# Token gathers of a mixture of experts take the list with out-of-range empty slots and skip them

## The chip, the cores and the metric

The kernel runs on one core of a Trainium2 chip. The metric is the time of one execution on the device in microseconds (us), measured over several runs; smaller is better. One further execution was taken with the hardware profiler, and all rows below come from it. The engines are PE (TensorE: matrix products), DVE (VectorE), ACT (ScalarE), POOL (GpSimd, which also issues all indirect transfers) and SP (SyncE, which issues the weight loads). Sixteen DMA engines move the data of all queues.

## What is computed

Two transformer blocks over 512 tokens of width 1024. The first has an attention mixer and then a mixture of 32 experts, of which each token uses four; the second block has another mixer. Nearly all weights, 384 pieces of 1 MB, belong to the experts. The part that matters here, cut from the reference:

```python
top_val, top_idx = lax.top_k(logits, TOP_K)          # TOP_K = 4 of 32 experts
gate = jax.nn.softmax(top_val, axis=-1)
...
u = hf[toks] @ w1[e] + b1[e]                         # hf: 512 x 1024, w1[e]: 1024 x 2048
g_, lin = u[:, :D_FF], u[:, D_FF:]
...
y = ((lin + 1.0) * g_ * jax.nn.sigmoid(SWIGLU_ALPHA * g_)) @ w2[e] + b2[e]
y = y * wts[:, None]
out = jax.ops.segment_sum(y.reshape(R, D), row_tok, num_segments=T)
```

## The kernel before

**Order of the experts.** Experts 0 and 1 come first, at fixed places. The other thirty are sorted on the chip by their number of tokens (`sort_keys`, `sorted_tables`). The fourteen fullest are "large" (kind `L`), with lists of 128 slots; the sixteen others are "small" (kind `S`), with at most 64 tokens. After the start, small and large ones alternate, so that one pair of experts is the period of the stage. `COL[e]` is the expert's column in the lists and `SLOTS[e]` the slots that its products use: 128 or 96 for a large one, 64 for a small one.

**Lists.** For each expert there is a column of token numbers, one slot in each partition. Filled slots come first, and the empty ones stand at the end. There are two versions. `ig` (large) and `igs` (small) are for the gather: an empty slot holds token 0. `isc` and `iscs` are for adding the result: an empty slot holds a row past the 512 tokens (512 + partition), and the tensor `accd` has 128 spare rows there. A small expert's 64 tokens are stored as 128 half rows: partitions 0 to 63 have the first 512 columns of the tokens, partitions 64 to 127 the second 512. Its lists count half rows, and its empty slots stand at the end of each half.

**Data flow of an expert e.** `gather(e)` on POOL (L1600) reads the rows of its tokens from `h2d` in HBM into the buffer `xg`. `turn_x(e)` transposes `xg` on PE (L1607 for large, L1629 for small ones) and copies the result out. `up(e)` multiplies with the first weights, `gated(e)` applies the gate, `turn_a(e)` transposes again, `down(e)` multiplies with the second weights, scales by the gate (0 for an empty slot) and adds the rows to `accd` with an indirect transfer on POOL that accumulates (L1737 large, L1708 small). There is one `xg`: in the middle of `up(e)`, at its step 4, `turn_x(e + 1)` empties it and right behind that `gather(e + 2)` is issued, about one expert ahead of its use. The first gather, `gather(1)`, is issued before the loop.

**Weights.** SP loads pieces of 1 MB (128 partitions of 8 KB, L135) as soon as a block of SBUF is free. Large experts' pieces are split into two parts, by ACT (L167) and DVE (L168), which then frees the block; small experts' pieces are used as they are.

Of the kernel before, what the change touches and what calls it, by code (L numbers as in the profile page):

```python
# [11 lines left out]
I32 = mybir.dt.int32  # L12
U32 = mybir.dt.uint32
AF = mybir.ActivationFunctionType
OP = mybir.AluOpType
# [4 lines left out]
P = 128  # L20
T = 512
# [14 lines left out]
NSMALL = 16  # L36
NWIDE = 4
NL = E - 2 - NSMALL
# [149 lines left out]
class Build:  # L188
# [912 lines left out]
    def middle(self):  # L1101
        nc, I, st, ar = self.nc, self.I, self.st, self.ar
        mm = nc.tensor.matmul
        c = self.const
# [42 lines left out]
        self.ig = c.tile([P, E], I32, name="ig")  # L1147
        self.isc = c.tile([P, E], I32, name="isc")

        self.igs, self.iscs = [c.tile([P, NSMALL], I32, name=n) for n in ("igs", "iscs")]  # L1150
        self.gates = c.tile([P, NSMALL], F32, name="gates")
        self.rank = c.tile([P, 1], F32, name="rank")

# [261 lines left out]
        ns = E - 2  # L1415
# [51 lines left out]
    def sorted_tables(self, pp):  # L1467

        nc = self.nc
        mm = nc.tensor.matmul  # L1470
        ns = E - 2
        y = pp.tile([P, D], F32, name="y", bufs=1)
        tu = self.sb_.cols(T, 2 * P)
        ones = self.halves[0:32, 0:1]

        def turned():
            nc.tensor.transpose(y[0:96, 0:P], self.tt, self.ident)
            nc.vector.tensor_copy(tu[0:96, 0:P], y[0:96, 0:P])
            nc.vector.tensor_copy(tu[0:96, P:].rearrange("p (h s) -> p h s", h=2),
                                  y[0:96, None, 0:64].to_broadcast([96, 2, 64]))  # L1480

        def by_rank():
            mm(y[:, 512:608], lhsT=tu[0:96, 0:P], rhs=self.bd[0:96, :], start=True, stop=True)
            mm(y[:, 608:704], lhsT=tu[0:96, P:], rhs=self.bd[0:96, :], start=True, stop=True)
            mm(y[0:1, 704:736], lhsT=self.pidf[0:32, :], rhs=self.bd[0:32, 0:E], start=True, stop=True)
            mm(y[0:1, 736:768], lhsT=ones, rhs=self.g[0:32, :], start=True, stop=True)
            nc.vector.tensor_copy(self.ids, y[0:1, 704:736])

        def lists():
            t, t2 = [y[:, a:a + 96].rearrange("p (c e) -> p c e", c=3) for a in (512, 608)]  # L1490
            f = self.sb_.cols(6 * T // 4 + 2 * E, NSMALL)

            nc.vector.tensor_scalar(f, t2[:, 1, NL:ns], -1.0, 1.0, op0=OP.mult, op1=OP.add)
            nc.vector.tensor_scalar(f, f, self.far2, self.half, op0=OP.mult, op1=OP.add)
            nc.vector.tensor_scalar(self.igs, t2[:, 0, NL:ns], 2.0, self.half, op0=OP.mult, op1=OP.add)
            nc.vector.scalar_tensor_tensor(self.iscs, t2[:, 0, NL:ns], 2.0, f, op0=OP.mult, op1=OP.add)
            nc.vector.tensor_copy(self.gates, t2[:, 2, NL:ns])
            self.slots(t[:, 0, :NL], t[:, 1, :NL], t[:, 2, :NL], self.sb_.cols(6 * T // 4 + 3 * E, NL), self.ig[:, :NL],
                       self.isc[:, :NL], self.gate[:, :NL])

        def slots():
            r, a, b = [self.sb_[0:1, 6 * T // 4 + o:6 * T // 4 + o + E] for o in (0, E, 2 * E)]
            nc.vector.tensor_copy(r, y[0:1, 736:768])
            nc.vector.tensor_scalar(a, r, float(NL), -32.0, op0=OP.is_ge, op1=OP.mult)
            nc.vector.tensor_scalar(b, r, float(NWIDE), -32.0, op0=OP.is_ge, op1=OP.mult)
            nc.vector.tensor_tensor(out=a, in0=a, in1=b, op=OP.add)
            nc.vector.tensor_scalar(r, r, float(ns), 64.0, op0=OP.is_ge, op1=OP.mult)
            nc.vector.tensor_tensor(out=a, in0=a, in1=r, op=OP.add)
            nc.vector.tensor_scalar(a, a, 128.0, None, op0=OP.add)
            nc.vector.tensor_copy(self.cap, a)  # L1510
            nc.vector.tensor_tensor(out=a, in0=self.cntf[0:1, :], in1=a, op=OP.subtract)
            nc.vector.tensor_scalar(a, a, 0.0, None, op0=OP.max)
            nc.vector.tensor_copy(self.over, a)
            nc.vector.tensor_reduce(out=self.top, in_=a, axis=AX.X, op=OP.max)
        return [turned, by_rank, lists, slots]

    def bias_rows(self, f):
# [28 lines left out]
    def experts(self):  # L1546
        nc, I, st, ar = self.nc, self.I, self.st, self.ar
        mm = nc.tensor.matmul
        with ExitStack() as cx:
# [14 lines left out]
            xg, s_ = [w[0].cols(q * D, D) for q in range(2)]  # L1564
# [4 lines left out]
            h2s, accs = [t[:, :].rearrange("t (h n) -> (t h) n", h=2) for t in (self.h2d, self.accd)]  # L1569

            def large(e):
                return KIND[e] == "L"
# [21 lines left out]
            def gather(e):  # L1594
                c = COL[e]
                if large(e):
                    out, src, ix = xg, self.h2d[0:T, :], self.ig[:, c:c + 1]
                else:
                    out, src, ix = xg[:, 0:T], h2s, self.igs[:, c - NL:c - NL + 1]
                nc.gpsimd.indirect_dma_start(out=out, out_offset=None, in_=src,  # L1600
                                             in_offset=bass.IndirectOffsetOnAxis(ap=ix, axis=0))

            def halves(e, at, H, L):
                n = SLOTS[e]
# [82 lines left out]
            def down(e):  # L1687
# [46 lines left out]
                if e == E - 1:  # L1734
# [3 lines left out]
                    out=self.accd, out_offset=bass.IndirectOffsetOnAxis(ap=self.isc[0:m, c:c + 1], axis=0),  # L1738
                    in_=ys[0:m, :], in_offset=None, compute_op=OP.add)

            it, self.sel = [self.gb.cols(D + q * T, T) for q in range(2)]
            gather(1)
            steps = self.sorted_tables(pp)
            st.span = 5
            for e in range(E + 1):
# [4 lines left out]
                if e < E:  # L1750
                    def hook(k):
                        if e == 0:
                            if k < len(steps):
                                steps[k]()
                            if k == 1:
                                st.stop = 1 << 30
                                st.pump()
                            if k == 2:
                                nc.scalar.preload_act_table_set("sigmoid_and_others")
                                for h in range(2):  # L1760
                                    nc.sync.dma_start(g2s[64 * h:64 * h + 64, :], self.modd[3:4, h * T:(h + 1) * T]
                                                      .to_broadcast([64, T]))
                            if k == 4:
                                turn_x(1)
                                gather(2)
                            return
                        if k == 1:
                            turn_a(e - 1)
                        if k == KD - 1 and e == E - 1:
                            nc.gpsimd.iota(it, pattern=[[1, T]], base=0, channel_multiplier=0,  # L1770
                                           allow_small_or_imprecise_dtypes=True)
                        if k == 4 and e + 1 < E:
                            turn_x(e + 1)
                            if e + 2 < E:
                                gather(e + 2)
# [3 lines left out]
                else:  # L1779
# [14 lines left out]
                    c = COL[e - 1]  # L1794
# [637 lines left out]
```

## Time and profile before

| what | us |
|---|---|
| runs | 1750.09, 1747.76, 1748.06 (median 1748.06) |
| the profiled execution's own time | 1749.42 |
| its span, first to last instruction | 1747.7 |
| PE busy | 1633.7 (93%) |
| DVE busy | 1070.9 (61%) |
| ACT busy | 821.8 (47%) |
| POOL busy | 376.8 (22%) |

The profiled execution's own time holds the span and 1.7 us around it. Busy time is the sum over an engine's instructions; PE's ends of matmuls are modelled, so a busy PE is not PE at its peak. A row of a transfer names its destination, then its source; "b" is any block of SBUF, `xg` among them.

### The profile page before, as it was taken

The page shows a single profiled execution, that of the slowest core. Times are in us where ns is not written, and L with a number is a line of the kernel's source. Part 1 is how long each engine was busy: PE and PEld are TensorE (multiplying, and loading weights), DVE is VectorE, ACT ScalarE, POOL GpSimd, SP SyncE. Part 2 cuts the span into 40 slices and gives each one's busy share as a digit, 9 for nine tenths or more (in the row PEclk, how much of TensorE's full clock was granted, in tenths as well). Part 3 has the DMA queues.
Part 4 walks back from the last instruction along what each step waited for, and adds up shares of the span by engine and source line. Part 5 has one row for each costly group of instructions (what it writes and reads, how often), then busy time and mean ns, then how long its engine had stood idle before and what let it go on. Part 6 is the DMA issues. An engine that isn't in the chain of part 4 may idle for free. (4 is left out here: it accounts for less than half of the span.)

```text
span 1747.7 us, 21964 instructions
## 1 busy us (share of the span) xinstructions
PE 1633.7 (93%) x7898; PEld 1046.9 (60%) x7899; DVE 1070.9 (61%) x1714; ACT 821.8 (47%) x1297; POOL 376.8 (22%) x259
## 2 busy tenths in 40 slices
PE   6999998897897999999999999999999989999998
PEld 4677755576742675565465464455455446778887
DVE  2567668668832475475485475476467486476653
ACT  4346568525521354254254255245245254477571
POOL 3012225222010120320321231231132130210120
PEclk9999999998999999999999999999999999999999
DMA  9812035467899999999999999999999986100301
GB/s 363 311 42 73 1 143 180 145 231 271 319 363 420 411 413 419 406 414 419 406 417 419 409 417 420 409 417 419 408 417 419 410 359 226 49 25 25 121 1 49
DMA packets 99975, 506.14 MB, mean 290 GB/s; under 512 B 10962, under 2 KB 20258, under 8 KB 48658
## 3 DMA queue, kind: packets, MB, share of 16 engines
q1 hardware_dynamic: 89972, 477.94, 67.1%
q0 software_dynamic: 9264, 25.68, 5.4%
q8 instruction: 64, 1.05, 0.2%
q10 hardware_dynamic: 624, 1.06, 0.2%
q14 instruction: 51, 0.42, 0.1%
HBM read 486.92 MB, written 17.71 MB: 289 GB/s over the span
## 5 line engine op out<-in xcount | busy, mean ns | idle before, releaser
L168 DVE TENSOR_TENSOR b<-b,b 128x1024 fp32r<-128x1024 f32 (+1 forms) x450 | 529.6, 1223 | 270.1 <-ACT b L167 269.4
L167 ACT CAST b<-b 128x1024 fp32r<-128x1024 f32 (+1 forms) x452 | 447.6, 1044 | 210.5 <-DMA b<-in_exp_w 168.7
L1737 POOL DMA_INDIRECT accd<-b,isc x15 | 154.9, 10325 | 405.3 <-DVE b L1732 388.5
L1590 PE MATMUL u<-b,b 128*64 128x512 f32 x1024 | 230.5, 597 | 0.3 <-DMA b<-in_exp_w 0.3
L257 PE MATMUL z<-b,b 128*128 128x512 f32 (+1 forms) x544 | 224.9, 414 | 2.9 <-ACT b L167 2.1
L258 PE MATMUL z<-b,b 128*128 128x512 f32 (+1 forms) x544 | 210.6, 387 | 1.5 <-DVE b L168 1.5
L257 PE MATMUL u<-b,b 128*96 128x512 f32 (+1 forms) x528 | 212.0, 401 | 0.0
L259 PE MATMUL z<-b,b 128*128 128x512 f32 (+1 forms) x544 | 210.6, 387 | 0.0
L259 PE MATMUL u<-b,b 128*96 128x512 f32 (+1 forms) x528 | 207.4, 393 | 0.0
L258 PE MATMUL u<-b,b 128*96 128x512 f32 (+1 forms) x528 | 207.4, 393 | 0.0
L1590 PEld LDWEIGHTS u<-b,b 128*64 128x64 f32 x1024 | 69.1, 136 | 129.2 <-issue 122.2
L257 PEld LDWEIGHTS z<-b,b 128*128 128x128 f32 x544 | 103.1, 190 | 33.4 <-issue 13.4
L258 PE MATMUL y<-b,b 128*96 128x512 f32 (+1 forms) x240 | 102.5, 427 | 18.5 <-DVE b L168 17.3
L1590 PE MATMUL y<-b,b 128*64 128x512 f32 x512 | 116.3, 605 | 0.8 <-DMA b<-in_exp_w 0.8
L259 PEld LDWEIGHTS z<-b,b 128*128 128x128 f32 x544 | 102.7, 189 | 21.9 <-DVE b L1929 0.4
L257 PE MATMUL y<-b,b 128*96 128x512 f32 (+1 forms) x240 | 100.6, 419 | 16.2 <-ACT b L167 16.2
L258 PEld LDWEIGHTS z<-b,b 128*128 128x128 f32 x544 | 103.3, 190 | 16.2 <-DVE b L168 2.5
L257 PEld LDWEIGHTS u<-b,b 128*96 128x96 f32 (+1 forms) x528 | 91.0, 172 | 35.2 <-ACT b L167 5.7
L259 PEld LDWEIGHTS u<-b,b 128*96 128x96 f32 (+1 forms) x528 | 90.8, 172 | 30.9
L258 PEld LDWEIGHTS u<-b,b 128*96 128x96 f32 (+1 forms) x528 | 90.9, 172 | 28.7 <-DVE b L168 0.2
L1609 ACT CAST b<-tr 128x768 fp32r<-128x768 f32 (+1 forms) x31 | 27.0, 871 | 157.8 <-PE tr L1607 155.3
L259 PE MATMUL y<-b,b 128*96 128x512 f32 (+1 forms) x240 | 98.8, 412 | 0.0
(516 smaller groups left out, 2098.5 us busy)
## 6 DMA issues: line engine op xcount, KB each, us to landing
b<-in_exp_w SPq DMA_DIRECT2D x384, 1024.0 KB, 20.8
b<-in_ada_w SPq DMA_DIRECT2D x24, 1024.0 KB, 5.7
b<-in_w_in SPq DMA_DIRECT2D x24, 1024.0 KB, 10.5
b<-in_w_out SPq DMA_DIRECT2D x8, 1024.0 KB, 4.9
b<-in_x SPq DMA_DIRECT2D x8, 512.0 KB, 7.3
b<-in_nsa_cmp_w POOLq DMA_DIRECT2D x2, 1024.0 KB, 8.8
b<-modd SPq DMA_DIRECT2D x4, 512.0 KB, 6.0
accd<-b SPq DMA_DIRECT2D x4, 512.0 KB, 4.5
```

Of the source, the lines that this page charges most:

```text
L167: nc.scalar.copy(hv, s)
L168: (other or nc.vector).tensor_tensor(out=lv, in0=s, in1=hv, op=OP.subtract)
L257: mm(out, lhsT=ah, rhs=bh, start=first, stop=False)
L258: mm(out, lhsT=ah, rhs=bl, start=False, stop=False)
L259: mm(out, lhsT=al, rhs=bh, start=False, stop=last)
L1590: mm(out[o, :], lhsT=lhsT, rhs=rhs[:, h * 512:(h + 1) * 512], start=False, stop=last, tile_position=(0, 64 * h), skip_group_check=True)
L1609: nc.scalar.copy(H[:, :, 0:n], pv)
L1737: nc.gpsimd.indirect_dma_start(out=self.accd, out_offset=bass.IndirectOffsetOnAxis(ap=self.isc[0:m, c:c + 1], axis=0), in_=ys[0:m, :], in_ ...
```

## The change

Gathers use the lists that the adds use, `isc` and `iscs`. They are given the number of the last valid row and told to pass over slots above it without an error, so nothing is read or written for an empty slot. `igs` and the instruction that made it go. `xg` is filled with zeros once, before the first gather, since rows of empty slots now keep what they held.

```diff
@@ middle
-        self.igs, self.iscs = [c.tile([P, NSMALL], I32, name=n) for n in ("igs", "iscs")]
+        self.iscs = c.tile([P, NSMALL], I32, name="iscs")
@@ sorted_tables, lists
-            nc.vector.tensor_scalar(self.igs, t2[:, 0, NL:ns], 2.0, self.half, op0=OP.mult, op1=OP.add)
@@ experts
             def gather(e):
                 c = COL[e]
                 if large(e):
-                    out, src, ix = xg, self.h2d[0:T, :], self.ig[:, c:c + 1]
+                    out, src, ix, n = xg, self.h2d[0:T, :], self.isc[:, c:c + 1], T
                 else:
-                    out, src, ix = xg[:, 0:T], h2s, self.igs[:, c - NL:c - NL + 1]
+                    out, src, ix, n = xg[:, 0:T], h2s, self.iscs[:, c - NL:c - NL + 1], 2 * T
                 nc.gpsimd.indirect_dma_start(out=out, out_offset=None, in_=src,
-                                             in_offset=bass.IndirectOffsetOnAxis(ap=ix, axis=0))
+                                             in_offset=bass.IndirectOffsetOnAxis(ap=ix, axis=0),
+                                             bounds_check=n - 1, oob_is_err=False)
...
+            nc.vector.memset(xg, 0.0)
             it, self.sel = [self.gb.cols(D + q * T, T) for q in range(2)]
             gather(1)
```

On DVE the filling stands between the sort of the experts and the first subtractions of the weights' split (L168). Before, around that place (`y` is the PSUM tile of the sorted tables):

```order
L1462 TENSOR_TENSOR b_3513<-b_3513 128x96
L1465 TENSOR_SCALAR b_3513<-b_3513,kc 128x32
L168 TENSOR_TENSOR b_3007<-b_3013,b_3007 128x1024
L168 TENSOR_TENSOR b_3008<-b_3013,b_3008 128x1024
L168 TENSOR_TENSOR b_3009<-b_3015,b_3009 128x1024
L168 TENSOR_TENSOR b_3010<-b_3015,b_3010 128x1024
L1478 COPY b_3513<-y 96x128
```

And with the change (`b_3664` is `xg`):

```order
L1462 TENSOR_TENSOR b_3512<-b_3512 128x96
L1465 TENSOR_SCALAR b_3512<-b_3512,kc 128x32
L1742 MEMSET b_3664 128x1024
L168 TENSOR_TENSOR b_3006<-b_3012,b_3006 128x1024
L168 TENSOR_TENSOR b_3007<-b_3012,b_3007 128x1024
L168 TENSOR_TENSOR b_3008<-b_3014,b_3008 128x1024
L168 TENSOR_TENSOR b_3009<-b_3014,b_3009 128x1024
L1478 COPY b_3512<-y 96x128
```

One instruction more stands ahead of the four subtractions and of L1478; everything behind keeps its order on DVE. On POOL, the first transfers of the stage before:

```order
L1600 DMA b_3665<-h2d,ig 128x1024 [waits DMAHW3_49,DMAHW2_49,DMAHW7_49,DMASW1_49,DVE_49]
L1600 DMA b_3665<-h2d,igs 128x512 [waits DMASW1_49,DMASW2_49,DVE_49,PE_49]
L1600 DMA b_3665<-h2d,igs 128x512 [waits DMASW3_49,DMASW2_49,PE_49]
L1737 DMA accd<-b_3666,isc 640x1024 [waits DMAHW1_49,DMAHW0_49,DMAHW4_49,DMASW4_49,DVE_49]
L1600 DMA b_3665<-h2d,igs 128x512 [waits DMASW3_49,PE_49]
```

And with the change:

```order
L1599 DMA b_3664<-h2d,isc 128x1024 [waits DMAHW2_49,DMAHW3_49,DMASW1_49,DMAHW7_49,DVE_49,PE_49]
L1599 DMA b_3664<-h2d,iscs 128x512 [waits DMASW1_49,DMASW2_49,DVE_49,PE_49]
L1599 DMA b_3664<-h2d,iscs 128x512 [waits DMASW3_49,DMASW2_49,PE_49]
L1737 DMA accd<-b_3665,isc 640x1024 [waits DMAHW1_49,DMAHW0_49,DMAHW4_49,DMASW4_49,DVE_49]
L1599 DMA b_3664<-h2d,iscs 128x512 [waits DMASW3_49,PE_49]
```

The order of gathers and adds on POOL is the same and the lists' names differ; the first gather's wait for DVE now covers the filling of `xg` too. PE, ACT and SP have the same rows as before.

## Rows read from the trace of the kernel before

**Rows 1.** The page, the span in forty equal slices of 43.7 us.
```profile
PE   6999998897897999999999999999999989999998
DMA  9812035467899999999999999999999986100301
```

**Rows 2.** DMA queues, 640 to 1360 us: packets, MB, share of 16 engines.
```profile
q1 hardware_dynamic: 38607, 281.15, 92.9%
q0 software_dynamic: 5427, 16.46, 8.5%
```

**Rows 3.** Waits of SP's queue, 640 to 1360 us: total us, times, longest.
```profile
SPq L135 <- DMA b<-in_exp_w: 498.5, 256, 3.9
```

**Rows 4.** Waits of PE, 640 to 1360 us.
```profile
PE y L258 <- DVE b L168: 15.7, 26, 0.8
PE y L257 <- ACT b L167: 15.2, 16, 2.0
```

**Rows 5.** POOL's timeline: start, us, instruction, idle before and its releaser.
```profile
412.96 1.14 POOL L1600 DMA_INDIRECT b<-h2d,ig  x1 [5.66 <-DVE empty L1428]
430.18 3.18 POOL L1600 DMA_INDIRECT b<-h2d,igs  x1 [16.08 <-DVE b L1512]
...
893.85 11.49 POOL L1737 DMA_INDIRECT accd<-b,isc  x1 [28.15 <-DVE b L1732]
905.65 1.54 POOL L1600 DMA_INDIRECT b<-h2d,ig  x1 [0.30 <-issue]
918.98 1.58 POOL L1708 DMA_INDIRECT accd<-b,iscs  x1 [11.78 <-DVE b L1707]
...
1356.62 1.55 POOL L1600 DMA_INDIRECT b<-h2d,ig  x1 [0.30 <-issue]
```

**Rows 6.** DMA queues, 523 to 528 us, with one large gather.
```profile
q1 hardware_dynamic: 218, 1.63, 77.1%
q0 software_dynamic: 144, 0.52, 25.6%
```

**Rows 7.** Busy time by window at the stage's end; the last two columns: DMA share, GB/s.
```profile
1429.50:1430.50 1.00, 0.00 (x0) 0.00 (x0) 1.00 (x2) 0.33 (x1) 0.00 (x0) 1.00 0.97 401
1430.50:1431.50 1.00, 0.00 (x0) 0.00 (x0) 0.96 (x2) 1.00 (x2) 0.00 (x0) 1.00 0.70 293
...
1433.00:1435.00 2.00, 1.00 (x7) 1.03 (x7) 2.00 (x3) 2.00 (x3) 0.00 (x0) 0.53 0.61 238
...
1436.00:1437.00 1.00, 1.00 (x4) 0.24 (x2) 1.00 (x2) 0.36 (x1) 0.00 (x0) 0.50 0.13 41
```

**Rows 8.** DVE's timeline at the stage's start.
```profile
415.10 4.62 DVE L168 TENSOR_TENSOR b<-b,b 128x1024 fp32r<-128x1024 f32 x4
419.64 0.28 DVE L1478 COPY b<-y 96x128 f32<-96x128 f32 x1
...
425.07 0.23 DVE L1495 TENSOR_SCALAR igs<-y,half 128x16 int32<-128x16 f32 x1
425.21 0.17 DVE L1496 SCALAR_TENSOR_TENSOR iscs<-y,b 128x16 int32<-128x16 f32 x1
```

**Rows 9.** Waits at the stage's start: PE, 400 to 500 us; SP's queue, 410 to 500 us.
```profile
PE y L1483 <- DVE b L1479: 1.0, 1, 1.0
...
SPq L135 <- DVE b L168: 55.2, 18, 11.7
```

**Rows 10.** POOL's timeline, its fillings of SBUF.
```profile
405.97 0.18 POOL L1447 MEMSET b<- 128x96 f32 x1
...
406.68 0.21 POOL L1450 MEMSET b<- 128x128 f32 x1
```

**Rows 11.** PE's timeline, two transposes of a gather; L1600, 640 to 1360 us, landing.
```profile
429.30 1.03 PE L1607 MATMUL tr<-ident,b 128*128 128x128 f32 x8
...
922.08 1.20 PE L1607 MATMUL tr<-ident,b 96*128 96x96 f32 x8
...
DMA to landing us min/median/max: 6.6/10.7/13.1
```

## The prediction

> **What bounds the kernel now.** I read the forty slices of the page first. From about 500 to 1400 us, the expert stage, the row of the DMA engines stands at 9 in every slice; PE stands at 9 too, so the slices alone don't say which of the two sets the pace [rows 1]. The DMA queues of 640 to 1360 us do: the weights' queue takes 92.9% and the GpSimd queue of gathers and adds 8.5% of sixteen engines, 101.4% together [rows 2]. Sums over 100% mean that packets overlap a little at their ends; no engine has a gap to fill. The issuing side agrees: SP's queue waits 498.5 of these 720 us for an earlier weight transfer to finish, so it is the transfers that hold the loads back and not a lack of free blocks [rows 3]. PE waits for pieces that ACT and DVE split, 15.2 and 15.7 us [rows 4], and those two have waited for weights. One pair of experts (small, then large) takes the time between two large gathers: (1356.62 - 905.65) / 7 = 64.4 us [rows 5], so the 720 us hold 11.2 pairs, and PE has (15.2 + 15.7) / 11.2 = 2.8 us of waiting in a pair. A stream that got faster by less than that would take PE with it.
>
> So the stage is bound by the engines' time, and the change takes work off exactly that. What a gather costs there is seen where a large one runs alone on its queue: in 523 to 528 us q0 has 144 packets (128 rows and 16 tiny ones for completion) in 25.6% of 16 x 5 us, which is 20.5 us or 0.16 us a row of 4 KB, and 128 x 0.16 / 16 = 1.28 us of all engines [rows 6]. A small gather has half the bytes, 0.64 us.
>
> **The change, part by part.** *Empty slots leave the gathers.* How many there are follows from the reference's seeded input (seed 0): the 30 sorted experts have 113, 102, 84, 81, 77, 77, 73, 71, 70, 68, 67, 66, 66, 64 tokens in the fourteen large lists and 62 down to 38 in the sixteen small ones. That leaves 713 of 14 x 128 rows empty in the large gathers and 196 row equivalents in the small: 909 rows, 909 x 0.16 / 16 = 9.1 us of all engines, if all sixteen got the same relief.
>
> They need not. A transfer is finished when its last engine is, and the engines aren't pooled: when the stage's queue runs dry the share of busy engines goes from 0.97 at 1430 us over 0.70 at 1431 and 0.61 at 1434 to 0.13 at 1436.5 [rows 7]. A third of them sit idle five microseconds before the last ones finish, and nobody takes over the rest. What counts is the relief of the engine that is relieved least. Empty slots stand together at the end of a list: in a large one from slot 64 or later on, in a small one from slot 38 or later of each half. The trace has no engine numbers, so how 128 slots are dealt to 16 engines must be bounded from both sides:
> - Dealt in blocks of slots (any blocks in which some engine has only low slots): that engine keeps its eight rows in every gather. Relief 0.
> - Dealt in turn (slot modulo 16): the fullest engine has a sixteenth of the list, rounded up. The large lists then save 0, 1, 2, 2, nine times 3 and 4 rows of 8, in sum 36, and the six small lists of at most 48 tokens one packet of 4 KB each: 42 x 0.16 = 6.7 us.
>
> I take 0. The row that speaks to it is [rows 6] again: while 128 gathered rows are being written into all partitions of xg, the weights' rows go into all partitions of another block, and the shares of the two queues make 77.1 + 25.6 = 102.7%, about what the weights have with the GpSimd queue over the long stretch. If the gathers' rows were dealt in another way than the weights' rows, engines would cross each other's partitions there, and I would expect stretched packets. So I read it that both are dealt alike, by partition, and then some engine has only low slots. This is an inference, and the 6.7 us stay in the range.
>
> [...]
>
> *A clearing of xg on DVE.* It stands ahead of four subtractions of L168, and DVE has no gap there from 415.10 on [rows 8]; PE then waits 1.0 us for L1479, and SP's queue 55.2 us in 410 to 500 us for blocks that L168 frees [rows 9]. So its whole time delays the start of the stream, before the engines are full. No row shows a clearing of 128x1024 on DVE. Lower bound: the copy of 96x128, 0.28 us; upper bound: a subtraction of 128x1024, 4.62 / 4 = 1.16 us [rows 8]. The nearest by operation are GpSimd's clearings, 0.18 us for 96 columns and 0.21 for 128 [rows 10], 0.9 ns for a column more, which gives 0.21 + 896 x 0.0009 = 1.0 us for 1024. I take 1.0. *The instruction for igs* goes: the next one started 0.14 us behind it [rows 8], so -0.14.
>
> *The first gather* now waits for the clearing: issue near 416.1 instead of 412.96 [rows 5]. Even with the longest landing of the full stage, 13.1 us [rows 11], it lands by 429.2, and PE transposes it at 429.30 [rows 11]; GpSimd has nothing else queued until 430.18 [rows 5]. Cost 0.
>
> *isc in the place of ig* makes the later gathers depend on instructions that ended by 426, while the second gather is issued at 430.18 [rows 5]. *The comparison with the bound* is work of GpSimd within L1600. No row shows it; I take 0 because a large gather now takes 1.5 us there, and one issued at 905.65 has until 922.08, when PE transposes it; with at most 13.1 us to landing, 3.3 us are spare [rows 5, 11]. Bounds: nothing, and 10 us (a rival, below).
>
> Sum: 0 + 1.0 - 0.14 = +0.9 us. The profiled execution took 1749.42 us and would take 1750.3; it lies 1.4 above the median of the runs shown, 1748.06, so the forecast for the median is 1748.06 + 0.9 = **1749.0 us**: no change that can be measured (0.2%, 3.5 us, is about what a measurement of this kernel can tell).
>
> **The rivals.**
> *The slots are dealt in turn.* Every engine is relieved, the stream gets 6.7 us shorter (9.1 at most), 0.5 us in a pair, which PE's 2.8 us of waiting takes along: 1749.0 - 6.7 = 1742.3, at most 1739.9. For it: the stage has no other bound, and every row saved would count. Against it: the sum of shares above.
> *The list's check is slow on GpSimd.* The adds are indirect transfers of the same size on the same engine and take 11.5 us in L1737 against 1.55 for a gather [rows 5]. If walking over skipped slots cost as much, a large gather would be issued 10 us longer, 3.3 are spare, and PE would wait 6.7 us in a pair, of which the 2.8 that it waits anyway are no loss: 13 x 3.9 = 51 us, 1800. It decides from 3.3 + 2.8 = 6.1 us more per gather on. Against it: a gather is not an add, and the small adds in L1708 take 1.58.
> *The change doesn't do what it says*: a skipped slot still costs the engine a packet. Then the sum is the same +0.9, and only the packets tell it from my forecast.
>
> **How the numbers follow.** Forecast (blocks) 0.62, no packets saved 0.05, dealt in turn 0.23, slow check 0.10. Faster by over 0.2% is the dealing in turn alone, 0.23; slower by over 0.2% the slow check, 0.10; within 0.2% the other two, 0.67. The range runs from 1741.0, which takes in the 6.7 us and most of what lies around them, to 1751.0: the upper bound of the clearing gives 1749.1, and 1.9 us are left for delays of the early stream. Outside lie the slow check and the far end of the even relief, somewhat under 2 in 10.
>
> **What would show it.** Right: q0's packets fall by about 700 rows of 4 KB and by some in the small gathers, the pair's period stays at 64.4 us, SP still waits for weights, but the sum of the shares in 640 to 1360 us falls under 100% since half of the engines run ahead and idle, and the drain at the end gets more uneven. Wrong: the period falls to 63.9 us with the shares still full (dealt in turn); or L1600 takes over 6 us and PE's L1607 waits for the gather (slow check); or q0 has as many packets as before (nothing skipped). A clearing far from 1.0 us, or PE not late at L1483, would put the small term wrong.

## The result, and the profile after

The changed kernel takes 1757.66 us (median of five runs, 1755.94 to 1759.96), the kernel before 1748.06: a ratio of 1.0056, with a 95% interval of 1.0044 to 1.0068. It is slower by 9.6 us. The forecast of 1749.0 us and its range of 1741 to 1751 are both missed, and "slower" had a chance of 0.10. The profiled execution took 1757.75 us with a span of 1756.0.

The gathers do what the diff says. Whole span, DMA packets and GpSimd's queue (packets, MB, share of 16 engines), first the kernel before:

```profile
DMA packets 99975, 506.14 MB, mean 290 GB/s; under 512 B 10962, under 2 KB 20258, under 8 KB 48658
q0 software_dynamic: 9264, 25.68, 5.4%
```

then the changed kernel:

```profile
DMA packets 99975, 502.16 MB, mean 286 GB/s; under 512 B 11927, under 2 KB 21223, under 8 KB 48658
q0 software_dynamic: 9264, 21.70, 5.0%
```

3.98 MB are no longer moved. That is 973 rows of 4 KB: the 909 of the prediction and the 64 empty slots of the first gather's list, which it had left out. But the number of packets is the same, 99975, and 965 more of them are under 512 B. So what is skipped leaves tiny packets behind. By the seeded counts they are one for each of the 777 empty rows of large gathers and one for each of 188 pairs of neighbouring empty half rows of small ones, 965 together; the trace has 777 packets of 4 bytes more than before and 188 of 8 bytes, where it had none.

So where did 9.6 us come from? DMA queues of the changed kernel, 640 to 1360 us, as in [rows 2]:

```profile
q1 hardware_dynamic: 38596, 281.09, 93.9%
q0 software_dynamic: 5408, 13.17, 7.5%
```

GpSimd's queue gave back 1.0 point of the engines' time, and the weights' queue took 1.0 point more, for the same 281 MB. The mean time of a weight packet follows from its share: 0.929 x 16 x 720 us / 38607 = 277.2 ns before, 0.939 x 16 x 720 us / 38596 = 280.3 ns after, 1.1% more. The change touches no weight load, yet on average they are slower. POOL's timeline, as in [rows 5] (start, us, instruction, idle before and its releaser):

```profile
417.51 1.28 POOL L1599 DMA_INDIRECT b<-h2d,isc  x1 [8.24 <-PE y L1477]
431.57 3.23 POOL L1599 DMA_INDIRECT b<-h2d,iscs  x1 [12.79 <-DVE b L1511]
...
909.76 1.59 POOL L1599 DMA_INDIRECT b<-h2d,isc  x1 [0.30 <-issue]
...
1363.26 1.61 POOL L1599 DMA_INDIRECT b<-h2d,isc  x1 [0.30 <-issue]
```

A pair of experts now takes (1363.26 - 909.76) / 7 = 64.79 us, against 64.42. A gather's instruction on POOL takes 1.6 us, as before, so no list is checked slowly. Waits, 640 to 1360 us, of SP's queue and of PE (total us, times, longest), as in [rows 3, 4]:

```profile
SPq L135 <- DMA b<-in_exp_w: 512.3, 254, 4.3
```

```profile
PE y L257 <- ACT b L167: 18.8, 13, 2.0
PE y L258 <- DVE b L168: 12.3, 20, 0.8
```

SP waits 13.8 us longer for weights, and PE as long as before for pieces. The stage is still bound by its transfers, and they are slower. Its end, as in [rows 7] (window, its length, busy time of five engines, granted clock, DMA share, GB/s):

```profile
1430.00:1432.00 2.00, 2.00 (x10) 1.32 (x8) 0.00 (x0) 0.00 (x0) 0.00 (x0) 1.00 1.05 332
1436.00:1438.00 2.00, 0.74 (x4) 0.00 (x0) 2.00 (x3) 0.32 (x1) 0.00 (x0) 1.00 0.44 182
1440.00:1442.00 2.00, 0.00 (x0) 0.00 (x0) 1.86 (x3) 2.00 (x3) 0.00 (x0) 0.77 0.31 126
1444.00:1446.00 2.00, 2.00 (x8) 0.55 (x8) 2.00 (x3) 0.80 (x1) 0.00 (x0) 0.50 0.09 29
```

More than half of the engines are done by 1437 us, and the last ones 8 us later; before, the share was down to 0.13 in 1436 to 1437. The relief falls to some engines and not to the slowest, as forecast. These are two separate things, then, an uneven relief and slower weights, and the experiments had to part them.

### The profile page after: what moved, and what is told of

It reads as the page before. It is cut to its first block, busy times and chain, and to the rows that moved or that the text cites. A ratio compares the mean times of both kernels' runs of the same rounds, so it can differ in the third digit from the quotient of the medians.

```text
span 1756.0 us, 21996 instructions
## 1 busy us (share of the span) xinstructions
PE 1637.8 (93%) x7898; PEld 1048.7 (60%) x7899; DVE 1070.6 (61%) x1714; ACT 822.2 (47%) x1297; POOL 371.1 (21%) x259
## 2 busy tenths in 40 slices
DMA packets 99975, 502.16 MB, mean 286 GB/s; under 512 B 11927, under 2 KB 21223, under 8 KB 48658
## 5 line engine op out<-in xcount | busy, mean ns | idle before, releaser
L168 DVE TENSOR_TENSOR b<-b,b 128x1024 fp32r<-128x1024 f32 (+1 forms) x450 | 529.2, 1222 | 277.9 <-ACT b L167 276.5
L1737 POOL DMA_INDIRECT accd<-b,isc x15 | 147.9, 9858 | 408.4 <-DVE b L1732 391.7
```

Source lines behind the costliest of these rows:

```text
L168: (other or nc.vector).tensor_tensor(out=lv, in0=s, in1=hv, op=OP.subtract)
L1737: nc.gpsimd.indirect_dma_start(out=self.accd, out_offset=bass.IndirectOffsetOnAxis(ap=self.isc[0:m, c:c + 1], axis=0), in_=ys[0:m, :], in_ ...
```

## The experiments

**1. The change and the kernel before, once more; the bound without skipping; fewer rows without a bound.** Both kernels were run again as they are. One run has only the bound:

```diff
+                                             bounds_check=n - 1, oob_is_err=False
```

with the old lists, which hold no row past the table. Another has no bound and lets a large gather fetch only the `SLOTS[e]` rows that are used:

```diff
-                    out, src, ix = xg, self.h2d[0:T, :], self.ig[:, c:c + 1]
+                    m = SLOTS[e]
+                    out, src, ix = xg[0:m, :], self.h2d[0:T, :], self.ig[0:m, c:c + 1]
```

Expected:

> The kernel before, unchanged, as a second program of its own. Theory 1 (skipping does it: the empty slots' engines run ahead, the sixteen engines drift apart and their weight packets stretch) and theory 2 (the tiny packets that skipped slots leave cost the engines time): ratio 1.000, weight packets at the pace of before, a pair of experts 64.4 us, last engine done about 1437 us. Theory 3 (the packets of every newly loaded program have their own pace, by where its data lie, and the change has nothing to do with it): the ratio may be anywhere within 0.995 to 1.006.

> The changed kernel once more. Theories 1 and 2: again 1.004 to 1.007, the pair at 64.8 us, a ragged drain that ends 8 us later than before. Theory 3: another ratio than 1.0056, down to 0.999, and packets that are not stretched.

> The bound is given to the gathers, but with the old lists, in which every empty slot has row 0, so nothing is skipped and nothing cleared. Theory 1 and theory 2: no change, 1.000, the drain as before. A fourth theory, that the form of the instruction with a bound is what costs: 1.005 like the change. Theory 3: anything.

> No bound; large gathers read only the 96 or 128 slots that their products use, so ten of the fourteen lists lose 32 rows, dealt evenly (six rows for each of sixteen engines instead of eight): 10 x 2 x 0.16 = 3.2 us less on every engine. Theory 1: the even relief is a gain, -3 us (0.998), no drift. Theory 2: -3 us too. If the stage were not bound by the engines: 0.

Measured: before again 1.0007 (0.9995 to 1.0018), the change again 1.0059 (1.0043 to 1.0076), the bound alone 1.0001 (0.999 to 1.0011), fewer rows 1.005 (1.0033 to 1.0066). So the loss comes back with the program, and checking a list costs nothing that can be told from zero. The fourth run is a miss, and a loss of its own, by another way: 0.998 was expected from six rows on each engine in place of eight, which was the author's assumption. Its DMA queues, 640 to 1360 us (in its quickest execution of six, 1750.19 us; the median is 1754.72):

```profile
q1 hardware_dynamic: 38364, 279.39, 93.0%
q0 software_dynamic: 5128, 15.24, 8.4%
```

1.22 MB less than before on GpSimd's queue free only 0.1 point of the engines, and the weights have 279.3 ns a packet. The trace has each packet's own time and size: in the same 720 us the gathers' packets of 4 KB take 176 ns on average in place of 159, and 935 of 34110 weight rows take over 330 ns, where the kernel before has 42 of 34333. So in this run the gathers of 96 rows have slower packets, and so have some of the weights beside them. Why is not shown; the trace has no engine numbers.

**2. Where the buffers lie.** In the changed kernel GpSimd's loads are already slower long before the first gather (rows below). What a removed instruction and a removed tile change there is the address of everything behind: `igs` has 64 bytes in each partition, and without it all blocks of SBUF that receive weights lie 64 bytes lower. In the compiled program the first starts at byte 24320 of its partition before, a multiple of 256, and at 24256 after. Four runs move the blocks. The change with a dead tile in the place of `igs`:

```diff
-        self.iscs = c.tile([P, NSMALL], I32, name="iscs")
+        self.pad, self.iscs = [c.tile([P, NSMALL], I32, name=n) for n in ("pad", "iscs")]
```

The kernel before with `igs` in unused columns of `ig`, which moves its blocks as the change does:

```diff
-        self.igs, self.iscs = [c.tile([P, NSMALL], I32, name=n) for n in ("igs", "iscs")]
+        self.igs = self.ig[:, NL:NL + NSMALL]
+        self.iscs = c.tile([P, NSMALL], I32, name="iscs")
```

The kernel before with 128 bytes more ahead of the blocks:

```diff
+        self.pad = c.tile([P, 32], I32, name="pad")
```

And the change without `ig`, which nothing in the gathers reads any more, and with `iscs` in unused columns of `isc`:

```diff
-        self.ig = c.tile([P, E], I32, name="ig")
...
-        self.iscs = c.tile([P, NSMALL], I32, name="iscs")
+        self.iscs = self.isc[:, NL:NL + NSMALL]
```

Expected:

> The change whole, with an unused tile of 64 bytes per partition where the tile igs stood, so that every buffer of the arena has the address again that it has in the kernel before (b0 at byte 24320 of its partition; 24256 in the change). Theory 'address' (the loss comes from the 64 bytes by which taking igs away moves the arena, and with it the destinations of all weight rows): ratio to the kernel before 0.998 to 1.001, the pair back at about 64.4 us, q1 back to about 92.9% between 640 and 1360 us, while the ragged end of the drain and the 965 packets under 512 B stay as in the change. Rival 'drift' (uneven skipping lets the DMA engines drift apart and this stretches packets) and rival 'tiny packets': ratio 1.005 to 1.006 as in the change, pair 64.8 us, q1 93.9%.

> The kernel before, with igs kept in unused columns of ig, so that its own 64 bytes are gone and the arena lies where it lies in the change (b0 at 24256). No gather skips anything, no bound, no clearing. Theory 'address': ratio 1.004 to 1.007, pair 64.8 us, q1 near 93.9% between 640 and 1360 us, end of the drain as even as before. Rivals 'drift' and 'tiny packets': ratio 0.999 to 1.001, pair 64.4 us.

> The kernel before with one more unused tile of 128 bytes per partition, so that the arena lies 128 bytes higher (b0 at 24448, 128 past a multiple of 256). Theory 'address' in the form that a row wants a start on a multiple of 256 bytes: ratio 1.004 to 1.007 as in the change. In the form that only multiples of 64 or 128 count: 0.999 to 1.001 (24448 is a multiple of 128, 24256 of 64 alone). Rivals 'drift' and 'tiny packets': 0.999 to 1.001.

> The change without the tile ig as well (nothing reads its lists of large experts any more), and with iscs in unused columns of isc: the arena lies at 24064, a multiple of 512. Two small instructions on VectorE fewer. Theory 'address': ratio 0.998 to 1.001, weight rows as fast as before or a little faster if multiples of 512 count more than those of 256. Rivals 'drift' and 'tiny packets': 1.005 to 1.006.

Measured:

| run | first block at | ratio | interval | q1, ns a packet |
|---|---|---|---|---|
| the change, padded | 24320 = 95 x 256 | 0.9996 | 0.9987 to 1.0005 | 277.5 |
| before, moved | 24256, 192 past a multiple | 1.0049 | 1.0036 to 1.0062 | 279.9 |
| before, 128 up | 24448, 128 past a multiple | 1.0055 | 1.0042 to 1.0068 | 279.6 |
| the change, no `ig` | 24064 = 94 x 256 | 0.9993 | 0.9984 to 1.0002 | 277.5 |

The last column is worked out as above, from the share of the weights' queue in 640 to 1360 us. For the padded change

```profile
q1 hardware_dynamic: 38899, 283.26, 93.7%
q0 software_dynamic: 5471, 13.43, 7.6%
```

and for the kernel before, moved,

```profile
q1 hardware_dynamic: 38279, 278.75, 93.0%
q0 software_dynamic: 5408, 16.39, 8.5%
```

Of the kernels whose queue was read in this window, the seven whose blocks start on a multiple of 256 have 277.1 to 277.5 ns, the run with gathers of 96 rows left aside (279.3), and the change and the two moved ones have 279.6 to 280.3.

This settles where the loss comes from. The kernel before, with not a byte of its gathers changed, loses about what the change lost when its blocks are moved, and the change loses nothing when they are moved back. The price fits too: 1.0% more (279.9 against 277.2) on 92.9% of the engines' time, over the some 930 us of the stage, is about 8.5 us; the moved kernel lost 0.0049 x 1747 = 8.6. The drift of engines and the tiny packets, the rivals, are out: the padded change has both and loses nothing.

The effect can be seen without any gather. GpSimd's queue in 40 to 80 us, where it carries loads for the first block's mixer and no token's row: before,

```profile
q0 software_dynamic: 576, 2.16, 14.1%
```

and before, moved:

```profile
q0 software_dynamic: 576, 2.16, 18.0%
```

The same 576 packets take 0.141 x 16 x 40 / 576 = 157 ns each, and 200 ns in the moved kernel. The changed kernel has 17.6% there, the one 128 up 17.7%, the padded change and the one without `ig` 14.1%.

Why the address counts is open. Packet by packet, it isn't that every transfer to such a start is slower. In 640 to 1360 us 32009 of 34333 weight rows of 8 KB take 309 ns in the kernel before; in the moved one 10553 of 34025 still do, and 21157 take 311 to 322 ns. The gathers' own packets of 4 KB go to a block that lies 64 bytes lower too, and they take 159 ns in both. A start 128 past a multiple costs as much as one 192 past, 279.6 and 279.9 ns a packet on average. No run shows the mechanism.

**3. Is the relief worth nothing, or on the wrong engines?** The padded change skips 973 rows and gains nothing that can be told from zero. Its stage is quicker in the middle: 283.26 MB of weights in the 720 us that held 281.15 before, and a pair takes (1354.92 - 905.63) / 7 = 64.18 us, against 64.42:

```profile
905.63 1.57 POOL L1599 DMA_INDIRECT b<-h2d,isc  x1 [0.30 <-issue]
...
1354.92 1.59 POOL L1599 DMA_INDIRECT b<-h2d,isc  x1 [0.30 <-issue]
```

The gain is gone at the end. Its windows there:

```profile
1426.00:1428.00 2.00, 1.56 (x8) 0.29 (x4) 2.00 (x3) 0.24 (x1) 0.00 (x0) 1.00 0.47 175
1430.00:1432.00 2.00, 0.00 (x0) 0.00 (x0) 1.90 (x2) 2.00 (x3) 0.00 (x0) 0.71 0.33 133
1434.00:1436.00 2.00, 2.00 (x8) 0.64 (x8) 2.00 (x3) 0.80 (x1) 0.00 (x0) 0.50 0.12 41
```

Half of the engines are idle some eight microseconds before the last ones finish. Two runs ask whether an even relief would count. One skips by partition: every fourth one is left out of every gather, with a token or without, through a mask that is added to the old lists. It leaves out a quarter of the tokens' rows, so it is not the whole computation and serves as a probe alone. Its blocks stay at 24320:

```diff
+        nc.vector.tensor_reduce(out=self.mk[:, 0:1], in_=self.ident.rearrange("p (a b) -> p b a", b=4)[:, 3, :],
+                                axis=AX.X, op=OP.add)
+        nc.vector.tensor_scalar(self.mk[:, 0:1], self.mk[:, 0:1], float(T), None, op0=OP.mult)
...
-        nc.vector.tensor_copy(ig, tok)
+        nc.vector.tensor_scalar(ig, tok, self.mk[:, 0:1], None, op0=OP.add)
...
```

The other is the change without `ig`, and deals out the slots of each list as the tables are turned:

```diff
-            nc.vector.tensor_copy(tu[0:96, 0:P], y[0:96, 0:P])
+            nc.vector.tensor_copy(tu[0:96, 0:96].rearrange("p (e r) -> p e r", e=12),
+                                  y[0:96, 0:96].rearrange("p (r e) -> p e r", e=12))
+            nc.vector.tensor_copy(tu[0:96, 96:P], y[0:96, 96:P])
...
```

The small lists are dealt out in the same way within each half, over 8 blocks.

Expected:

> The change with the arena at 24320 as in the kernel before, but the slots passed over are chosen by partition and not by emptiness: every fourth partition (3, 7, 11, ...) of every gather is skipped, whether it holds a token or not, and empty slots in the other partitions are fetched as before. It leaves out a quarter of the tokens' rows (3.1 MB, against 3.98 MB that the change leaves out). Adds are untouched. Theory 'wrong engines' (the stage follows its most loaded DMA engines, and the empty slots at the end of each list relieve only some of them): 768 rows' worth of 4 KB, at 0.2 us each and dealt over 16 engines, take some 10 us from every engine, so the ratio is 0.993 to 0.997 although fewer bytes are left out than in the change. Rival 'the gathers' bytes don't bound the stage': 0.999 to 1.001, as the change with the arena restored.

> The change without ig (arena at 24064), and the order of the slots of the sorted experts is dealt out: consecutive slots of a list go to partitions 8 apart, within the first 96 partitions for the large experts and within each half of 64 for the small ones, by the access pattern of the copies that turn the tables. The result is the whole computation. Three copies of 0.3 us in place of two on VectorE. Theory 'wrong engines': empty slots now relieve engines 0 to 11 as well, by the empties within the caps, a smaller part than a fourth of the rows: 0.996 to 0.999, below the 0.9993 of the change without ig, and a more even end of the drain. Rival 'bytes don't bound': 0.999 to 1.001.

Measured: skipped by partition 0.9963 (0.995 to 0.9976); dealt out 1.0008 (0.9999 to 1.0018). The first leaves out fewer bytes than the change and is 6.5 us faster by its ratio, where the padded change gained 0.7. Its packets, whole span:

```profile
DMA packets 99976, 503.13 MB, mean 289 GB/s; under 512 B 11443, under 2 KB 20739, under 8 KB 48659
```

That is 3.01 MB less than before, 736 rows' worth against 973; the expectation's 768 had one large gather too many. At 0.16 us a row [rows 6] 736 rows are 7.4 us of every engine, if they fall evenly on sixteen, and 6.4 once 1 us goes for the clearing, close to what was measured; the expectation's 0.2 us a row was too much. The pair of experts shrinks to (1351.62 - 903.77) / 7 = 63.98 us:

```profile
903.77 1.59 POOL L1606 DMA_INDIRECT b<-h2d,ig  x1 [0.30 <-issue]
...
1351.62 1.59 POOL L1606 DMA_INDIRECT b<-h2d,ig  x1 [0.30 <-issue]
```

In its last microseconds the engines end nearly as close together as before [rows 7], and earlier:

```profile
1426.00:1428.00 2.00, 0.00 (x0) 0.00 (x0) 1.90 (x2) 2.00 (x3) 0.00 (x0) 0.87 0.68 282
1430.00:1432.00 2.00, 2.00 (x7) 0.72 (x8) 2.00 (x3) 0.80 (x1) 0.00 (x0) 0.50 0.20 73
```

So bytes do bound the stage, and the empties at the end of a list are, as these two runs have it, on the wrong engines. The second run is a miss: 0.996 to 0.999 was expected, and the end is as ragged as the change's, with some two engines of sixteen (a share of 0.12 to 0.13) at work from 1432 to 1440 us:

```profile
1430.00:1432.00 2.00, 0.00 (x0) 0.00 (x0) 2.00 (x3) 0.63 (x1) 0.00 (x0) 1.00 0.21 87
1432.00:1434.00 2.00, 0.00 (x0) 0.00 (x0) 1.86 (x3) 2.00 (x3) 0.00 (x0) 1.00 0.13 53
1434.00:1436.00 2.00, 0.80 (x5) 0.83 (x6) 2.00 (x2) 2.00 (x3) 0.00 (x0) 0.65 0.12 49
1436.00:1438.00 2.00, 2.00 (x9) 0.96 (x9) 2.00 (x3) 1.00 (x2) 0.00 (x0) 0.50 0.12 41
1438.00:1440.00 2.00, 2.00 (x6) 0.47 (x4) 2.00 (x3) 0.00 (x0) 0.00 (x0) 0.50 0.12 10
```

**4. The place within a block of eight.** That run put each list's empties at partitions whose number modulo 8 is high. If anything is dealt by a finer rule than blocks of eight, such an order is uneven again. So slots go on a diagonal: slot 12k + b of a large list to partition 8b + (k + b) mod 8, by way of a doubled copy that is read with a stride of 15.

```diff
+                for t in range(2):
+                    nc.vector.tensor_copy(w[:, 0:2 * n].rearrange("p (e t r) -> p t e r", t=2, r=8)[:, t],
+                                          y[0:96, 0:n].rearrange("p (r e) -> p e r", r=8))
+                for o, at, m in out:
+                    nc.vector.tensor_copy(tu[0:96, o:o + 8 * m].rearrange("p (e r) -> p e r", r=8),
+                                          w[:, at:at + 15 * m].rearrange("p (e r) -> p e r", r=15)[:, :, 0:8])
...
```

The same order was also given to the kernel before, with its old lists, as a control. Expected:

> As the run with the empties dealt out, but consecutive slots of a sorted list go to partitions 8 apart and also to different places within the block of 8 (slot k*12+b of a large expert to partition 8b + (k+b) mod 8, slot k*8+b of a small one to 8b + (k+b) mod 8), by five more small copies on VectorE (some 1 us). The result is the whole computation. Theory 'two dealings' (a gather gives each engine a block of 8 partitions, an add of rows gives them to the engines in turn, partition mod 16; the run before put the empties at the same places of every block, which took the adds' relief, which the kernel before has at every engine, away from those engines whose number mod 8 is low): now both are even, and the most loaded engine is relieved by some 5 to 6 us against the kernel before: ratio 0.996 to 0.998. Rival 'the dealing itself costs' or 'the gain of the even skips came only from the tokens left out': 0.999 to 1.002, no better than the change without ig.

> The kernel before with the same order of slots and its old lists, nothing skipped by a gather, no bound, no clearing, arena at 24320. Theory 'two dealings': every gather fetches all its rows, so all engines keep that load; only the adds' empty slots move, from even to even: 0.999 to 1.001. If the order of the slots pays by itself, without skipping: below 0.998.

Measured: the diagonal 0.9981 (0.9971 to 0.9991), 1743.95 us, a hair outside the 0.996 to 0.998 that was expected; the control 1.0004 (0.9994 to 1.0014). The order alone pays nothing, skipping alone pays nothing that can be told from zero, and both together are 3.3 us faster by the ratio than the kernel before. This version beats both kernels. Against the change without `ig` (0.9993), which it is built on, the gain is 2.1 us, and the two intervals overlap. The period of a pair tells them apart: (1353.31 - 905.80) / 7 = 63.93 us, against (1353.24 - 904.03) / 7 = 64.17 without `ig` and 64.18 in the padded change:

```profile
905.80 1.57 POOL L1608 DMA_INDIRECT b<-h2d,isc  x1 [0.30 <-issue]
...
1353.31 1.59 POOL L1608 DMA_INDIRECT b<-h2d,isc  x1 [0.30 <-issue]
```

The last microseconds of its stage:

```profile
1430.00:1432.00 2.00, 2.00 (x10) 1.29 (x11) 2.00 (x3) 1.45 (x2) 0.00 (x0) 0.50 0.30 114
1432.00:1434.00 2.00, 2.00 (x8) 0.64 (x6) 2.00 (x2) 0.12 (x1) 0.00 (x0) 0.50 0.09 32
```

Why the place within eight matters is open. The expectation's reading is that adds are dealt to the engines in turn, and that the run before took their relief from some. The traces speak against it, since adds have no relief to lose. Packet by packet, the large adds of 640 to 1360 us have 1185 packets of 4 KB, with a median of 327 ns, in the kernel before, in the padded change and on the diagonal, and 1186 in the run that was dealt out: the rows of empty slots are added too, at full price.

How the gathers' rows might be dealt to the engines can be tried on the seeded counts. If it is by blocks of eight partitions, the engine that is relieved least gets 0 rows in the change, 28.5 in the run that was dealt out, 28.5 on the diagonal and 46 when every fourth partition is skipped, in estimates at 0.16 us a row [rows 6] 0, 4.6, 4.6 and 7.4 us. Once 1 us is taken off for the clearing and up to 1 more for the copies, three runs are near it and the dealt-out one is not: -0.7 (padded), +1.4, -3.3 and -6.5 us were measured against the kernel before, each give or take 1.6 to 2.3 us. If it is in turn, slot modulo 16, the change itself should have had 46 rows (the prediction's 42 and four of the first gather) or 7.4 us, and the skip of every fourth partition none. So neither of the two fits all four. What the dealing is, no run shows: the trace has no engine numbers.

## Why the prediction was wrong

**The step that failed** is "*The instruction for igs* goes: the next one started 0.14 us behind it [rows 8], so -0.14". It priced an instruction, and what goes with it is a tile. Its 64 bytes move every block by 64 bytes, and all 384 MB of weights are then written to rows that don't start on a multiple of 256. That term is +8.6 us (before, moved) where -0.14 stood; between the padded change and the change as it is there are some 10 us, the same within the intervals. With the tile's place kept, the change measures 0.9996, or -0.7 us with an interval of -2.3 to +0.9, and the forecast's +0.9 is the upper end of that. None of the rivals had it: each was about the gathers.

**Dealt in blocks, relief 0**: right for the change as far as the runs can tell. That some engine has only low slots was the author's inference; the trace has no engine numbers to show it. The padded run's interval, less the 0.9 us of the small terms, leaves a relief of 0 to 3.2 us and excludes the 6.7 of dealing in turn; its end is ragged, and an even relief (skipped by partition) pays at once. The inference from the sum of the shares was sound in its result, though no run shows that engines which cross each other's partitions stretch packets; and blocks of eight neighbours would have given the dealt-out run 4.6 us, where it measured 1.4 us slower.

**The sum of the shares falls under 100%**: wrong. It stays at 101.4% in the change and is 101.3% when padded. As I read it, relieved engines don't idle in the stage; they run ahead with the weights as far as the free blocks reach (64.18 us a pair in the padded run, against 64.42), and the lead is lost at the end, where the last engine counts.

**The clearing of xg, 1.0 us**: right. DVE's timeline of the changed kernel, to be held against [rows 8]:

```profile
415.34 0.23 DVE L1465 TENSOR_SCALAR b<-b,kc 128x32 f32<-128x32 f32 x1
415.73 0.91 DVE L1742 MEMSET b<- 128x1024 f32 x1 [0.16 <-issue]
416.56 4.56 DVE L168 TENSOR_TENSOR b<-b,b 128x1024 fp32r<-128x1024 f32 x4
```

0.91 us, and the first subtraction starts 1.22 us behind L1465; before, it started 0.14 behind it (414.96 and 415.10), so the chain is 1.08 us longer. With -0.14 for `igs` the small terms come to what was forecast for them.

**The first gather, cost 0**: right. It was issued at 417.51, later than the 416.1 that was forecast, and PE's first transpose of it began 15.35 us behind the start of L1465 in the changed kernel and 15.35 in the padded one, against 14.34 before; that one microsecond is the clearing. PE's timeline of the changed kernel, as in [rows 11]:

```profile
430.69 1.03 PE L1607 MATMUL tr<-ident,b 128*128 128x128 f32 x8
```

**The comparison with the bound, 0**: right, by the run with the bound alone (1.0001) and by 1.6 us for a gather. The rival of the slow check is out.

**A skipped slot still costs a packet**: true by count, 99975 packets in both, if tiny ones, and it was wrong to call an equal count the sign that nothing is skipped. The bytes and the share of the queue are the sign: 13.17 MB in 7.5%, against 16.46 in 8.5% [rows 2].

## What to carry to other kernels

A tile that a change removes is also an address that it moves: before an edit is priced by its instructions, compare where the buffers behind it start. In this kernel the starts on multiples of 256 bytes were the quick ones, 277.1 to 277.5 ns a weight packet against 279.6 to 280.3, so try those for the targets of large loads. Where a stage is bound by its sixteen DMA engines, as here, ask where the saved bytes fall: 973 rows skipped at the ends of the lists were worth 0.7 us, which can't be told from zero, 736 skipped at every fourth partition 6.5. Look at the drain, the time in which the stage's queue runs dry, for how many engines are left, and try other ways to deal the saving out over the partitions: one gained nothing here (1.0008), the diagonal 3.3 us. A control that moves addresses alone costs one dead tile and separates the two at once.

## What was not expected of the hardware

- **A block 64 bytes lower or 128 higher made loads slower.** Weight packets took 279.6 to 280.3 ns on average in place of 277.2, the packets of GpSimd's queue at 40 to 80 us 196 to 200 in place of 157, and the kernel 0.5% more. But 31% of the weight rows in the moved kernel and 34% in the changed one took 309 ns as before, and the gathers' packets 159. Only these starts were tried: multiples of 256, 128 past and 192 past. Whether 32 or 64 past a multiple cost as much is open, and so is the mechanism.
- **A gather of 96 rows cost more a row than one of 128.** In the run that has them the gathers' packets of 4 KB took 176 ns in place of 159. With 1.22 MB less the queue freed 0.1 point, and the kernel lost 0.5%, as much as by the address, though its blocks had not moved; rows were cheaper to skip (0.9996, padded) than to cut off (1.005).
- **Skipped slots leave packets of 4 and 8 bytes**: 965 more under 512 B, at an equal count. The dealt-out run has 905 more and the diagonal 869, as the counts of rows and of pairs of half rows would have it.
- **An add moves the rows of its empty slots at full price**: 1185 or 1186 packets of 4 KB at a median of 327 ns, whatever the gathers skip.
